# Scores in two passes, decay from two parts of g, later GpSimd constants and a store on a second queue: one hybrid attention layer

## Chip, cores and metric

One Trainium2 chip, one NeuronCore of it. The metric is the device time of one execution in microseconds (us); the kernel before has a median of 174.89 us over three runs (174.42 to 174.91).

## What is computed

One decoder layer on x of 256 tokens by 1024 columns, all in float32. After an RMS norm, one projection `h @ w_in` (1024 by 4104) gives ten parts. Eight softmax heads of 64 columns use the first four:

```
logit = q . k * 64**-0.5 - slope[h] * distance        # causal, 256 tokens
moba_out = softmax(logit) @ v * silu(a_z)
```

Four gated-delta heads of 128 columns use the rest. `g = -exp(a_log) * softplus(d_a + dt_bias)` is the log decay, `gc` its running sum, and `decay[i, j] = exp(gc[i] - gc[j])` for j not after i enters a triangular solve and a recurrence over the sequence. Both results, the second normed and gated, are joined and go through `w_out` (1024 by 1024); a last RMS norm and `x +` give the output.

## The kernel before, in words

**Precision by parts.** A float32 operand is split into a high part, rounded as it is written as float32r by ScalarE (ACT), and the low rest, made by VectorE (DVE). A product is then three TensorE (PE) passes of float32r: high by high, high by low, low by high. Weight groups of 512 columns come by DMA into four `raw` buffers, are split into `hi` and `lo` tiles (five buffers each), and feed the projections `dz`, `dk`, `dq`, `dv`, `av`, `aq`, `ak`, `az` and then `out` in that program order.

**The planner.** Nothing is emitted directly. Every operation is recorded (all have line 372 in the profile, so one goes by the tiles' names), and `Plan.run` list-schedules them by modelled durations; the best of eight rounds is the order in which each engine gets its instructions. `LEAD` is added to the priority of the operations of a stage; `BATCH` to that of a PE operation on the same rows as the one before it. Operations marked `late` (48 dummy `ps_warm` matmuls) go where the model finds PE without other work.

**The head** (L474 to L587). GpSimd (POOL) makes masks and other constants: `ident`, `ones`, `triu`, `blk`, `blks`, `strl`, `lvl`, `bias0`, `qscale`, zeros in `yz16` and in the `qz` tiles. For each half t of the tokens ACT squares 512 columns of x and DVE the other 512, each with a sum; DVE adds the two sums and EPS (L571); POOL raises that to -0.5 (L572, `raise_to`); ACT and DVE scale x (L573, L574); PE transposes it into `hT`, from which `hhi` and `hlo` are made. `dz` is the first projection.

**The decay** (L713 to L729). `gs` is `triu` times g of each head, 128 by 512 per chunk t, in float32. PE multiplies it by `strl` in float32 and adds the causal mask (`far16`, bf16) into `ps_d`; ACT makes `dT`, its exponential.

**The scores** (L976 to L1016). A query pair m has a tile `qz` with its high and its low part; each head e owns 64 of the 128 rows, and the other 64 are zeros written by POOL, so that PE contracts over 128 rows though only 64 count. The keys' parts `ka_h`, `ka_l` are 128 rows for both heads of a pair. Each head has two blocks of scores, of 128 and of 256 columns, and three matmuls for each:

```
PE.matmul(o, qh[:, ts], kh[:, m, ks], start=True, stop=False)
PE.matmul(o, qh[:, ts], kl[:, m, ks], start=False, stop=False)
PE.matmul(o, ql[:, ts], kh[:, m, ks], start=False, stop=True)
```

**The end** (L1102 to L1126). Squares and sums of `ps_out`, a power on POOL, then per column group a DVE operation and a store, all stores on SyncE's (SP's) queue: two groups for the first 128 tokens, three for the last 128.

Of the kernel before, what the change touches and what calls it, by code (L numbers as in the profile page):

```python
# [123 lines left out]
class Plan:  # L124
# [24 lines left out]
    def record(self, eng, real, name, args, kw):  # L149
        op = Op()  # L150
# [14 lines left out]
        after = kw.pop("after", False)  # L165
# [212 lines left out]
SLACK = 20  # L378

SWITCH = 90  # L380
BATCH = 0

MARGIN = [411, 175, 0]
TABLE = 2000
# [10 lines left out]
def tile_hybrid(  # L395
# [17 lines left out]
    plan = Plan()  # L413
# [4 lines left out]
    def const(shape, name, dtype=F32):  # L418
        return plan.tile(sb, shape, dtype, name)
# [4 lines left out]
    def sl(tag, shape, name, dtype=F32):  # L424
        return plan.tile(sb, shape, dtype, name, tag=tag)
# [14 lines left out]
    HD = D // 2  # L440
# [29 lines left out]
    HB = [P, HG, P]  # L470
# [9 lines left out]
    ones = const([P, P], "ones")  # L480
    G.memset(ones, 1.0)

    for t in range(NT):
        G.memset(yz16[:, of_chunk[t], :], 0.0)
# [4 lines left out]
    blk = const([P, NB, BASE], "blk")  # L489
    G.memset(blk, 1.0)  # L490
    G.affine_select(out=blk, in_=blk, pattern=[[-BASE, NB], [0, BASE]], compare_op=OP.is_ge,
                    fill=0.0, base=0, channel_multiplier=1)
    G.affine_select(out=blk, in_=blk, pattern=[[BASE, NB], [0, BASE]], compare_op=OP.is_ge,
                    fill=0.0, base=BASE - 1, channel_multiplier=-1)

    blks = const([P, NB, BASE], "blks")
    G.affine_select(out=blks, in_=blk, pattern=[[BASE, NB], [1, BASE]], compare_op=OP.is_gt,
                    fill=0.0, base=0, channel_multiplier=-1)
# [7 lines left out]
    V.tensor_scalar(far16, strl, -NEG, None, op0=OP.mult)  # L506
# [4 lines left out]
    nl = P // (2 * BASE)  # L511
    lvl = const([P, nl, 2, BASE], "lvl")
    G.memset(lvl[:, :, 0, :], 0.0)
    G.memset(lvl[:, :, 1, :], 1.0)
    G.affine_select(out=lvl[:, :, 1, :], in_=lvl[:, :, 1, :], pattern=[[-2 * BASE, nl], [0, BASE]],
                    compare_op=OP.is_ge, fill=0.0, base=0, channel_multiplier=1)
    G.affine_select(out=lvl[:, :, 1, :], in_=lvl[:, :, 1, :], pattern=[[2 * BASE, nl], [0, BASE]],
                    compare_op=OP.is_ge, fill=0.0, base=BASE - 1, channel_multiplier=-1)


    bias0 = const([P, P + T], "bias0")
    G.iota(bias0[:, :P], pattern=[[1, P]], base=0, channel_multiplier=-1,
           allow_small_or_imprecise_dtypes=True)
    G.affine_select(out=bias0[:, :P], in_=bias0[:, :P], pattern=[[-1, P]], compare_op=OP.is_ge,
                    fill=NEG, base=0, channel_multiplier=1)
    G.iota(bias0[:, P:], pattern=[[1, T]], base=-P, channel_multiplier=-1,
           allow_small_or_imprecise_dtypes=True)
    G.affine_select(out=bias0[:, P:], in_=bias0[:, P:], pattern=[[-1, T]], compare_op=OP.is_ge,
                    fill=NEG, base=P, channel_multiplier=1)
    slopes = [2.0 ** -(h + 1) for h in range(HA)]  # L530

    qscale = const([P, HA // 2], "qscale")
    for h in range(HA):
        b = DA * (h % 2)
        G.memset(qscale[b : b + DA, h // 2 : h // 2 + 1], (DA ** -0.5) / slopes[h])
# [29 lines left out]
    for t in range(NT):  # L565
        junk = sl(f"s{1 + t}", [P, D], f"xsq{t}")
        A.activation(junk[:, :HD], xs[t][:, :HD], AF.Square, scale=D ** -0.5, accum_out=ssq[:, t, 0:1])
        V.tensor_tensor_reduce(junk[:, HD:], xs[t][:, HD:], xs[t][:, HD:], 1.0 / D, 0.0, op0=OP.mult, op1=OP.add,
                               accum_out=ssq[:, t, 1:2])
        r = rx[:, t : t + 1]  # L570
        V.tensor_scalar(r, ssq[:, t, 0:1], ssq[:, t, 1:2], EPS, op0=OP.add, op1=OP.add)  # L571
        raise_to(r, r, -0.5, [P, 1])  # L572
        A.activation(xs[t][:, :HD], xs[t][:, :HD], AF.Copy, scale=r)  # L573
        V.tensor_scalar(xs[t][:, HD:], xs[t][:, HD:], r, None, op0=OP.mult)  # L574
# [409 lines left out]
    sm = const([P, HA, 2], "sm")
    rs = const([P, HA, 2], "rs")
# [4 lines left out]
    kps = proj_group(512, "ak")  # L990
    for half in range(2):
        plan.stage = f"att{half}"
        ps = qps[half]
        for c in range(2):
            m = 2 * half + c
            for e in range(2):
                b = slice(DA * e, DA * e + DA)
                qs_ = qscale[b, m : m + 1]
                qh, ql = qz[m][b, 0, e, :], qz[m][b, 1, e, :]
                A.activation(qh, ps[b, c, :], AF.Copy, scale=qs_)  # L1000
                V.scalar_tensor_tensor(ql, ps[b, c, :], qs_, qh, op0=OP.mult, op1=OP.subtract)
        ps = kps[half]
        hm = slice(2 * half, 2 * half + 2)
        A.activation(kh[:, hm, :], ps, AF.Copy)
        V.tensor_tensor(kl[:, hm, :], ps, kh[:, hm, :], OP.subtract)
# [102 lines left out]
    for t in range(NT):  # L1108
        n = len(groups[t])
        pq = tmp("pq", [P, n], f"pq{t}")  # L1110
        u = uu[:, t, :]
        r = tmp("pr", [P, 1], f"pr{t}")

        for i, (c0, cn) in enumerate(groups[t]):
            cs = slice(c0, c0 + cn)
            A.activation(osj[:, i % 2, :cn], accs[t][i], AF.Square, scale=D ** -0.5, accum_out=pq[:, i : i + 1])
            if i:
                V.tensor_scalar(r, pq[:, i : i + 1], r, None, op0=OP.add)
            else:
# [3 lines left out]
        for c0, cn in groups[t]:  # L1123
# [32 lines left out]
```

## Time and profile before

| | us |
|---|---|
| profiled execution | 174.88 |
| its span, first to last instruction | 172.9 |
| median of 3 runs | 174.89 |
| PE busy | 164.1 (95%) |
| DVE busy | 134.7 (78%) |
| ACT busy | 108.8 (63%) |
| POOL busy | 21.2 (12%) |

A matmul's own duration in the profile overlaps with the next one's, since they are pipelined; what PE needs for one is read from the distance of the starts, or from a piece of the chain of waits divided by its count. A float32 matmul shows as two records, a float32r or bf16 one as one. The shape shown for a matmul is that of the weights' rows and columns, then the moving operand's.

### The profile page before, as it was taken

Reading aid. Unit: us, or ns where it says so; the run is one execution under the profiler, and the core shown is the slowest. Engines: PE = TensorE matmul, PEld = TensorE weight load, DVE = VectorE, ACT = ScalarE, POOL = GpSimd, SP = SyncE. Lnnn points to the kernel's source line nnn. Section 1 sums busy time; section 2 is a strip of 40 time slices with the busy share of each in tenths; the row PEclk is TensorE's granted clock in tenths of the full one; section 3 lists DMA queues with packets and bytes.
Section 4 is the critical chain, followed back from the end, with each engine's and each line's share of the span. In section 5 each row is a group of like instructions: output and inputs, shape, how many; then the busy total and the mean of one; then the engine's idle time right before and its main releaser. Section 6 shows DMA issues by size and latency. Waiting matters only on the chain.

```text
span 172.9 us, 3465 instructions
## 1 busy us (share of the span) xinstructions
PE 164.1 (95%) x1311; PEld 154.1 (89%) x1311; DVE 134.7 (78%) x330; ACT 108.8 (63%) x231; POOL 21.2 (12%) x58
## 2 busy tenths in 40 slices
PE   7799999999999999999999999999999999999950
PEld 5589999997999999989999999999999998888850
DVE  4589566799579999898798999999689676474542
ACT  3689949968785545478554575665849594671230
POOL 8950000000000300400020000000001810000110
PEclk9999999999999999999999999999999999999995
DMA  5667689995776351067676108600000000640033
GB/s 193 232 224 261 224 271 241 391 317 136 207 233 161 91 189 57 5 205 276 222 245 200 69 0 251 238 0 0 8 0 4 2 0 0 196 172 0 3 118 121
DMA packets 12326, 24.92 MB, mean 144 GB/s; under 512 B 741, under 2 KB 1046, under 8 KB 12310
## 3 DMA queue, kind: packets, MB, share of 16 engines
q1 hardware_dynamic: 12310, 24.71, 44.1%
q8 instruction: 10, 0.16, 0.4%
q14 instruction: 6, 0.05, 0.1%
HBM read 23.65 MB, written 1.05 MB: 143 GB/s over the span
## 4 chain that ended last, share of the span: by engine, by line
PE 87%; POOL 5%; issue 4%; ACT 1%; DVE 1%; POOLq 0%; DVEq 0%
PE ps_out L372 10%; PE ps_av L372 9%; PE ps_az L372 7%; PE ps_dz L372 7%; PE ps_ak L372 7%; PE ps_dq L372 7%; PE ps_aq L372 7%; PE ps_dv L372 7%; PE ps_dk L372 7%; PE ps_s L372 3%; PE ps_y L372 2%; PE ps_w L372 2%; PE ps_gb L372 2%; PE ps_pt L372 2%; PE ps_d L372 1%
## 5 line engine op out<-in xcount | busy, mean ns | idle before, releaser
L372 DVE TENSOR_TENSOR o_lo<-raw_o,o_hi 128x1024 fp32r<-128x1024 f32 x8 | 9.8, 1220 | 5.1 <-ACT o_hi L372 5.1
L372 ACT ACTIVATE o_hi<-raw_o 128x1024 fp32r<-128x1024 f32 x8 | 8.4, 1056 | 5.0 <-PE ps_az L372 2.7
L372 ACT ACT_TABLE_LOAD x8 | 10.3, 1283 | 0.9 <-PEq L1143 0.8
L372 ACT ACTIVATE att_y<-att_y,mx 128x128 f32<-128x128 f32 (+1 forms) x16 | 7.2, 448 | 4.4 <-DVE mx L372 4.4
L372 PE MATMUL ps_az<-hlo,az_hi 128*128 128x256 f32 x32 | 9.8, 305 | 0.0
L372 PE MATMUL ps_az<-hhi,az_lo 128*128 128x256 f32 x32 | 9.6, 300 | 0.0
L372 PE MATMUL ps_aq<-hlo,aq_hi 128*128 128x256 f32 x32 | 9.6, 299 | 0.0
L372 PE MATMUL ps_az<-hhi,az_hi 128*128 128x256 f32 x32 | 9.5, 297 | 0.0
L372 PE MATMUL ps_warm<-wz 128*128 128x256 bf16 x48 | 8.3, 333 | 1.1 <-DVE wz L372 1.1
L372 PE MATMUL ps_aq<-hhi,aq_hi 128*128 128x256 f32 x32 | 9.3, 291 | 0.0
L372 PE MATMUL ps_aq<-hhi,aq_lo 128*128 128x256 f32 x32 | 9.2, 291 | 0.0
L372 PE MATMUL ps_dq<-hlo,dq_hi 128*128 128x256 f32 x32 | 9.1, 286 | 0.0
L372 PE MATMUL ps_dq<-hhi,dq_lo 128*128 128x256 f32 x32 | 9.1, 289 | 0.0
L372 PE MATMUL ps_ak<-hhi,ak_lo 128*128 128x256 f32 x32 | 9.1, 284 | 0.0
L372 PE MATMUL ps_ak<-hhi,ak_hi 128*128 128x256 f32 x32 | 9.1, 284 | 0.0
L372 PE MATMUL ps_dv<-hlo,dv_hi 128*128 128x256 f32 x32 | 9.1, 283 | 0.0
L372 PE MATMUL ps_dq<-hhi,dq_hi 128*128 128x256 f32 x32 | 9.0, 283 | 0.0
L372 PE MATMUL ps_dk<-hhi,dk_hi 128*128 128x256 f32 x32 | 9.0, 286 | 0.0
L372 PE MATMUL ps_dv<-hhi,dv_lo 128*128 128x256 f32 x32 | 9.0, 280 | 0.0
L372 PE MATMUL ps_ak<-hlo,ak_hi 128*128 128x256 f32 x32 | 9.0, 280 | 0.0
L372 PE MATMUL ps_dv<-hhi,dv_hi 128*128 128x256 f32 x32 | 9.0, 280 | 0.0
L372 PE MATMUL ps_dk<-hlo,dk_hi 128*128 128x256 f32 x32 | 8.9, 280 | 0.0
(254 smaller groups left out, 635.6 us busy)
## 6 DMA issues: line engine op xcount, KB each, us to landing
raw_o<-in_w_out_dram SPq DMA_DIRECT2D x4, 1024.0 KB, 5.0
raw_dz<-in_w_in_dram SPq DMA_DIRECT2D x8, 260.0 KB, 8.1
raw_dk<-in_w_in_dram SPq DMA_DIRECT2D x2, 1024.0 KB, 9.3
raw_dq<-in_w_in_dram SPq DMA_DIRECT2D x2, 1024.0 KB, 12.9
raw_dv<-in_w_in_dram SPq DMA_DIRECT2D x2, 1024.0 KB, 9.4
raw_av<-in_w_in_dram SPq DMA_DIRECT2D x2, 1024.0 KB
raw_aq<-in_w_in_dram SPq DMA_DIRECT2D x2, 1024.0 KB, 5.9
raw_ak<-in_w_in_dram SPq DMA_DIRECT2D x2, 1024.0 KB, 7.1
```

The costliest lines, as they stand in the source:

```text
L372: op.call(*args, **kw)
```

## The change

Six parts. The queries' high part of a head stays on its own 64 rows and its low part goes to the other 64; the keys' high part is written on both halves, so one matmul over 128 rows gives high by high and low by high together, and a second one with the keys' low part (zeros on the other half) the third product. `g` is split into two float32r parts, and the decay is two float32r matmuls for each chunk. POOL's constants that later stages use (`blk`, `blks`, `lvl`, `bias0`, `qscale`, the zeros in `yz16` and in the low keys) are the same operations as at the head before, now recorded after the `dz` stage, with a dependence on its last operation. The sum of the two square sums moves from DVE to POOL, with EPS as start of DVE's sum. The store of the second column group goes on ACT's queue. The planner's numbers are other ones.

```diff
-            op.preds[self.ops[-1]] = True
+            op.preds[after if isinstance(after, Op) else self.ops[-1]] = True
...
-BATCH = 0
+BATCH = 752
...
-LEAD = {"out0": 3258, "dk": 2097, "inv": -3594, "av": 2525, "dbl": -402, "out1": -1204, "att0": -470, "mixd": -508, "az": -1375}
+LEAD = {"out0": 3258, "dk": 12754, "inv": -3594, "dbl": -402, "out1": -1204, "att0": -192, "mixd": 1425, "az": -11589, "dz": -5411, "gates": 158, "vt": -3052}
...
-    strl = const([P, P], "strl")
+    strl = const([P, P], "strl", F32R)
...
-        V.tensor_tensor_reduce(junk[:, HD:], xs[t][:, HD:], xs[t][:, HD:], 1.0 / D, 0.0, op0=OP.mult, op1=OP.add,
+        V.tensor_tensor_reduce(junk[:, HD:], xs[t][:, HD:], xs[t][:, HD:], 1.0 / D, EPS, op0=OP.mult, op1=OP.add,
                                accum_out=ssq[:, t, 1:2])
         r = rx[:, t : t + 1]
-        V.tensor_scalar(r, ssq[:, t, 0:1], ssq[:, t, 1:2], EPS, op0=OP.add, op1=OP.add)
+        G.tensor_tensor(r, ssq[:, t, 0:1], ssq[:, t, 1:2], OP.add)
...
+    now = plan.ops[-1]
+    blk = const([P, NB, BASE], "blk")
+    G.memset(blk, 1.0, after=now)
+    G.affine_select(out=blk, in_=blk, pattern=[[-BASE, NB], [0, BASE]], compare_op=OP.is_ge,
+                    fill=0.0, base=0, channel_multiplier=1, after=now)
...
+    for t in range(NT):
+        G.memset(yz16[:, of_chunk[t], :], 0.0, after=now)
...
-    gsa = sl("ms", HBB, "gs")
+    gpart = [const(GS, f"g{i}", F32R) for i in "hl"]
+    A.activation(gpart[0], gneg, AF.Copy)
+    V.tensor_tensor(gpart[1], gneg, gpart[0], OP.subtract)
+    gsa = [sl(g, HBB, f"gs{g}", F32R) for g in ("ms", "wT")]
...
-        gs = gsa[:, of_chunk[t], :]
-        V.tensor_tensor(gs, triu[:, None, :].to_broadcast(HB), gneg[:, t, :, None].to_broadcast(HB), OP.mult)
-        PE.matmul(pd, strl, gs, start=True, stop=False)
+        for i in range(2):
+            gs = gsa[i][:, of_chunk[t], :]
+            V.tensor_tensor(gs, triu[:, None, :].to_broadcast(HB), gpart[i][:, t, :, None].to_broadcast(HB), OP.mult)
+            PE.matmul(pd, strl, gs, start=i == 0, stop=False)
...
+            G.memset(kl[own[1 - e], e, :].bitcast(F32), 0.0, after=now)
...
+    own = [slice(DA * e, DA * e + DA) for e in range(2)]
...
+            q, kh, kl = sets[m]
...
+                b, b2 = own[e], own[1 - e]
...
-                A.activation(qh, ps[b, c, :], AF.Copy, scale=qs_)
-                V.scalar_tensor_tensor(ql, ps[b, c, :], qs_, qh, op0=OP.mult, op1=OP.subtract)
-        A.activation(kh[:, hm, :], ps, AF.Copy)
-        V.tensor_tensor(kl[:, hm, :], ps, kh[:, hm, :], OP.subtract)
...
+                A.activation(q[b, e, :], ps, AF.Copy, scale=qs_)
+                V.scalar_tensor_tensor(q[b2, e, :], ps, qs_, q[b, e, :], op0=OP.mult, op1=OP.subtract)
+                ps = kps[half][b, c, :]
+                A.activation(kh[b, e, :], ps, AF.Copy)
+                A.activation(kh[b2, e, :], ps, AF.Copy)
+                V.tensor_tensor(kl[b, e, :], ps, kh[b, e, :], OP.subtract)
...
-                    PE.matmul(o, qh[:, ts], kh[:, m, ks], start=True, stop=False)
-                    PE.matmul(o, qh[:, ts], kl[:, m, ks], start=False, stop=False)
-                    PE.matmul(o, ql[:, ts], kh[:, m, ks], start=False, stop=True)
+                    PE.matmul(o, q[:, ts], kh[:, ks], start=True, stop=False)
+                    PE.matmul(o, q[:, ts], kl[:, ks], start=False, stop=True)
...
-            SP.dma_start(out[0, t * P : (t + 1) * P, cs], u[:, cs])
+            (AQ if i == 1 else SP).dma_start(out[0, t * P : (t + 1) * P, cs], u[:, cs])
```

## Rows read from the trace of the kernel before

**Rows 1.** The page's shares of the span by engine in the chain of work that ended last, and all that the view of waits gives for PE: who waited for whom, us in total, times, longest.

```profile
PE 87%; POOL 5%; issue 4%; ACT 1%; DVE 1%; POOLq 0%; DVEq 0%
PE hT L372 <- ACT x L372: 1.7, 2, 1.3
PE ps_warm L372 <- DVE wz L372: 1.1, 1, 1.1
```

**Rows 2.** Busy time of each engine in stretches of the span (start and end in us, the length, busy us and instructions of each engine, granted clock, DMA share, GB/s).

```profile
24.00:48.00 24.00, 24.00 (x195) 22.69 (x193) 19.34 (x41) 20.26 (x29) 0.00 (x0) 1.00 0.87 258
48.00:92.00 44.00, 44.00 (x333) 41.81 (x333) 40.00 (x93) 27.49 (x59) 4.60 (x5) 1.00 0.53 168
92.00:134.00 42.00, 42.00 (x425) 41.22 (x424) 38.91 (x115) 27.14 (x71) 0.76 (x4) 1.00 0.23 77
134.00:149.00 15.00, 15.00 (x115) 14.17 (x114) 9.06 (x19) 9.73 (x21) 4.46 (x9) 1.00 0.03 8
```

**Rows 3.** The chain of waits from 99 to 116 us: start, length, what.

```profile
103.30 0.70 PE ps_s L372 x6
...
108.77 0.53 PE ps_s L372 x5
...
110.27 1.02 PE ps_y L372 x32
```

**Rows 4.** PE in order of time: the decay's matmuls (start, length, what), and two neighbours of 512 columns in float32r.

```profile
40.52 1.02 PE L372 MATMUL ps_d<-gs,strl 128*128 128x512 f32 x2
41.38 0.38 PE L372 MATMUL ps_d<-far,ident 128*128 128x512 bf16 x1
...
159.55 0.40 PE L372 MATMUL ps_out<-o_lo,mixa_hi 128*128 128x512 f32 x1
159.78 0.39 PE L372 MATMUL ps_out<-o_hi,mixa_lo 128*128 128x512 f32 x1
```

**Rows 5.** POOL in order of time at the head.

```profile
5.52 0.99 POOL L372 MEMSET yz<- 128x512 f32 x2
6.47 0.57 POOL L372 TENSOR_TENSOR rx<-rx,pow-1_88 128x1 f32<-128x1 f32 x1
7.77 0.65 POOL L372 TENSOR_SCALAR_AFFINE_SELECT bias<-bias 128x128 f32<-128x128 f32 x2
8.39 1.08 POOL L372 TENSOR_TENSOR rx<-rx,pow-1_88 128x1 f32<-128x1 f32 x1
```

**Rows 6.** ACT and DVE in order of time at the head.

```profile
4.72 0.19 ACT L372 ACTIVATION_READ_ACCUMULATOR xsq<-x 128x1 f32 x1
5.00 0.21 DVE L372 TENSOR_SCALAR rx<-ssq 128x1 f32<-128x1 f32 x1
6.20 0.19 ACT L372 ACTIVATION_READ_ACCUMULATOR xsq<-x 128x1 f32 x1
7.07 0.72 ACT L372 ACTIVATE x<-x,rx 128x512 f32<-128x512 f32 x1 [0.69 <-POOL rx L372]
7.47 0.21 DVE L372 TENSOR_SCALAR rx<-ssq 128x1 f32<-128x1 f32 x1
9.51 0.72 ACT L372 ACTIVATE x<-x,rx 128x512 f32<-128x512 f32 x1 [0.55 <-POOL rx L372]
```

**Rows 7.** PE in order of time at the head.

```profile
7.85 1.16 PE L372 MATMUL hT<-ident,x 128*128 128x128 f32 x8 [1.29 <-ACT x L372]
10.44 1.13 PE L372 MATMUL hT<-ident,x 128*128 128x128 f32 x8 [0.39 <-ACT x L372]
...
23.87 0.72 PE L372 MATMUL ps_warm<-wz 128*128 128x256 bf16 x5
```

**Rows 8.** Groups of instructions by shape, on POOL, DVE and ACT: count, busy us, mean ns of one, idle before.

```profile
L372 POOL TENSOR_TENSOR om<-om,sq 128x4 f32<-128x4 f32 x4 | 0.8, 203 | 0.2
L372 POOL TENSOR_SCALAR_AFFINE_SELECT blks<-blk 128x128 f32<-128x128 f32 x1 | 0.8, 833 | 0.0
L372 DVE TENSOR_TENSOR gs<-triu,gneg 128x512 f32<-128x512 f32 x2 | 1.3, 683 | 0.0
L372 DVE TENSOR_TENSOR ka_l<-ps_ak,ka_h 128x512 fp32r<-128x512 f32 x2 | 1.4, 692 | 0.1
L372 DVE TENSOR_TENSOR u<-ps_out,wpost 128x256 f32<-128x256 f32 x2 | 0.8, 418 | 0.5 <-ACT osj L372 0.5
L372 ACT ACTIVATE avT<-ps_av 64x256 f32<-64x256 f32 x8 | 3.0, 372 | 2.5 <-PE ps_av L372 2.5
```

**Rows 9.** In order of time: ACT's last gate activations of `dz`, and DVE's first use of `blks`.

```profile
30.50 0.94 ACT L372 ACTIVATE zt<-ps_dz 128x256 f32<-128x256 f32 x3
...
63.20 1.28 DVE L372 TENSOR_TENSOR msk<-bT,blks 128x512 f32<-128x512 f32 x2
```

**Rows 10.** The end: PE's last matmul in order of time, and the last two pieces of the chain.

```profile
166.57 0.28 PE L372 MATMUL ps_out<-o_hi,mixa_lo 128*128 128x256 f32 x1
169.09 0.40 DVEq L1152
169.48 0.40 DVE u L372
```

**Rows 11.** The matmuls of `az` alone in a stretch (length, PE busy and count, clock, DMA share, GB/s), and DVE's making of their low parts, by shape.

```profile
100.00:134.00 34.00, 8.17 (x42) 1.00 0.19 64
L372 DVE TENSOR_TENSOR az_lo<-raw_az,az_hi 128x1024 fp32r<-128x1024 f32 x4 | 4.9, 1214 | 0.0
```

More of the change, by code (lines that the diff above doesn't have):

```diff
@@ L481, in tile_hybrid @@
     G.memset(ones, 1.0)
-    for t in range(NT):
-        G.memset(yz16[:, of_chunk[t], :], 0.0)
     triu = const([P, P], "triu")
@@ L487, in tile_hybrid @@
                     fill=0.0, base=0, channel_multiplier=-1)
[L489 to L498, printed above, removed]
-    strl = const([P, P], "strl")
+    strl = const([P, P], "strl", F32R)
     G.affine_select(out=strl, in_=ones, pattern=[[-1, P]], compare_op=OP.is_gt,
@@ L505, in tile_hybrid @@
     far16 = const([P, P], "far16", BF16)
-    V.tensor_scalar(far16, strl, -NEG, None, op0=OP.mult)
+    V.tensor_scalar(far16, strl.bitcast(F32), -NEG, None, op0=OP.mult)
     emod = const([P, BASE], "emod")
     V.tensor_reduce(emod, ident.rearrange("p (b k) -> p k b", k=BASE), op=OP.add, axis=AX.X)
[L511 to L535, printed above, removed]
     power = {}
@@ L668, in tile_hybrid @@
         A.activation(A_[t], z0[:, t, :], AF.Silu)
+    now = plan.ops[-1]
[3 more added lines that the diff above has]
+                    fill=0.0, base=0, channel_multiplier=1, after=now)
+    G.affine_select(out=blk, in_=blk, pattern=[[BASE, NB], [0, BASE]], compare_op=OP.is_ge,
+                    fill=0.0, base=BASE - 1, channel_multiplier=-1, after=now)
+    blks = const([P, NB, BASE], "blks")
+    G.affine_select(out=blks, in_=blk, pattern=[[BASE, NB], [1, BASE]], compare_op=OP.is_gt,
+                    fill=0.0, base=0, channel_multiplier=-1, after=now)
+    nl = P // (2 * BASE)
+    lvl = const([P, nl, 2, BASE], "lvl")
+    G.memset(lvl[:, :, 0, :], 0.0, after=now)
+    G.memset(lvl[:, :, 1, :], 1.0, after=now)
+    G.affine_select(out=lvl[:, :, 1, :], in_=lvl[:, :, 1, :], pattern=[[-2 * BASE, nl], [0, BASE]],
+                    compare_op=OP.is_ge, fill=0.0, base=0, channel_multiplier=1, after=now)
+    G.affine_select(out=lvl[:, :, 1, :], in_=lvl[:, :, 1, :], pattern=[[2 * BASE, nl], [0, BASE]],
+                    compare_op=OP.is_ge, fill=0.0, base=BASE - 1, channel_multiplier=-1, after=now)
+    bias0 = const([P, P + T], "bias0")
+    G.iota(bias0[:, :P], pattern=[[1, P]], base=0, channel_multiplier=-1,
+           allow_small_or_imprecise_dtypes=True, after=now)
+    G.affine_select(out=bias0[:, :P], in_=bias0[:, :P], pattern=[[-1, P]], compare_op=OP.is_ge,
+                    fill=NEG, base=0, channel_multiplier=1, after=now)
+    G.iota(bias0[:, P:], pattern=[[1, T]], base=-P, channel_multiplier=-1,
+           allow_small_or_imprecise_dtypes=True, after=now)
+    G.affine_select(out=bias0[:, P:], in_=bias0[:, P:], pattern=[[-1, T]], compare_op=OP.is_ge,
+                    fill=NEG, base=P, channel_multiplier=1, after=now)
+    slopes = [2.0 ** -(h + 1) for h in range(HA)]
+    qscale = const([P, HA // 2], "qscale")
+    for h in range(HA):
+        b = DA * (h % 2)
+        G.memset(qscale[b : b + DA, h // 2 : h // 2 + 1], (DA ** -0.5) / slopes[h], after=now)
+    for t in range(NT):
+        G.memset(yz16[:, of_chunk[t], :], 0.0, after=now)
     vh = const([P, NT, HA * DA], "vh", F32R)
@@ L975, in tile_hybrid @@
     avT = sl("s4", [P, HA // 2, T], "avT")
-    qz = [plan.tile(sb, [P, 2, 2, T], F32R, f"qz{m}", tag=g) for m, g in enumerate(("qz", "s3", "s2"))]
-    qz.append(qz[0])
-    for q in qz[:3]:
+    SET = [P, 2, 2, T]
+    q01 = const(SET, "qz", F32R)
+    k0, k1 = sl("s3", SET, "k0", F32R), sl("s2", SET, "k1", F32R)
+    qk2, kl2 = const(SET, "qk2", F32R), const([P, 2, T], "kl2", F32R)
+    sets = [(q01[:, 0], k0[:, 0], k0[:, 1]), (q01[:, 1], k1[:, 0], k1[:, 1]), (qk2[:, 0], qk2[:, 1], kl2)]
+    sets.append(sets[0])
+    own = [slice(DA * e, DA * e + DA) for e in range(2)]
+    for _, _, kl in sets[:3]:
         for e in range(2):
-            G.memset(q[DA * (1 - e) : DA * (2 - e), :, e, :].bitcast(F32), 0.0)
-    kh = const([P, HA // 2, T], "ka_h", F32R)
-    kl = const([P, HA // 2, T], "ka_l", F32R)
+            G.memset(kl[own[1 - e], e, :].bitcast(F32), 0.0, after=now)
     mx = const([P, HA, 2], "mx")
@@ L992, in tile_hybrid @@
         plan.stage = f"att{half}"
[L993 removed]
         for c in range(2):
             m = 2 * half + c
+            q, kh, kl = sets[m]
             for e in range(2):
[L997 to L1005 removed]
+                b, b2 = own[e], own[1 - e]
+                ps, qs_ = qps[half][b, c, :], qscale[b, m : m + 1]
+                A.activation(q[b, e, :], ps, AF.Copy, scale=qs_)
[4 more added lines that the diff above has]
+                V.tensor_tensor(kl[b, e, :], ps, kh[b, e, :], OP.subtract)
         for pr2 in range(2):
@@ L1010, in tile_hybrid @@
                 h = 2 * m + e
-                qh, ql = qz[m][:, 0, e, :], qz[m][:, 1, e, :]
+                q, kh, kl = (v[:, e, :] for v in sets[m])
                 ps_s = bank([P, P + T], f"ps_s{h}")
                 for o, ts, ks in ((ps_s[:, :P], slice(0, P), slice(0, P)), (ps_s[:, P:], slice(P, T), slice(0, T))):
-                    PE.matmul(o, qh[:, ts], kh[:, m, ks], start=True, stop=False)
-                    PE.matmul(o, qh[:, ts], kl[:, m, ks], start=False, stop=False)
-                    PE.matmul(o, ql[:, ts], kh[:, m, ks], start=False, stop=True)
+                    PE.matmul(o, q[:, ts], kh[:, ks], start=True, stop=False)
+                    PE.matmul(o, q[:, ts], kl[:, ks], start=False, stop=True)
                 y = tmp("att_p", [P, P + T], f"att_y{h}")
@@ L1122, in tile_hybrid @@
         raise_to(r, r, -0.5, [P, 1])
-        for c0, cn in groups[t]:
+        for i, (c0, cn) in enumerate(groups[t]):
             cs = slice(c0, c0 + cn)
             V.scalar_tensor_tensor(u[:, cs], u[:, cs], r, xr[:, t, cs], op0=OP.mult, op1=OP.add)
-            SP.dma_start(out[0, t * P : (t + 1) * P, cs], u[:, cs])
+            (AQ if i == 1 else SP).dma_start(out[0, t * P : (t + 1) * P, cs], u[:, cs])
     plan.emit(psum)
```

## The prediction

> **What bounds the kernel now.** I read first the chain that ended last and PE's waits. PE is 87% of the chain, and the only waits of PE that the profile finds are two at its very start, for the scaled x and for the dummy operand [rows 1]. Then I cut the span into stretches: from 24 to 149 us PE is busy without a gap [rows 2]. A busy PE alone proves little, as matmuls overlap in the records; what proves it is the distance of the starts, which the chain shows: six score matmuls in a row take 0.70 us, 32 small ones 1.02 us, and one group follows on the other [rows 3]. So the time is: the head until PE is fed, PE's queue, and a tail after the last matmul. What shortens PE's queue shortens the kernel, as long as nobody feeds PE later. The engine to watch is DVE: 38.91 of 42 us busy between 92 and 134 us, 40.00 of 44 before that, but only 9.06 of 15 behind it [rows 2]. ACT has room everywhere.
>
> The sum is made on the profiled execution, 174.88 us: its span of 172.9 and 2.0 around it, which I leave as it is. It lies 0.01 under the median, so no correction is needed.
>
> **Scores in two passes.** Eight heads times two blocks lose one matmul each: 16. In the chain, runs of five and six of them, half of 128 and half of 256 columns, take 0.53 and 0.70 us [rows 3], 0.106 to 0.117 us each. 16 x 0.117 = 1.87 us off PE; the low end by these rows is 16 x 0.106 = 1.70. The Trainium skill ("TensorE: Matmul & The Clock Gate", section "Back-to-back issue gap") gives about 81 ns for a sustained matmul of 128 columns and 109 ns for 256 by its formula; by that the part would be worth 8 x 0.190 = 1.52 us, an estimate from the page. The rows stand above it, and I go by the rows; by the page the result below would be 0.35 us later.
>
> **Decay.** A chunk's float32 product takes from 40.52 to 41.38 us, 0.86 us for its two records; a float32r matmul of 512 columns is 0.23 us from the next one's start [rows 4]. Two of these are 0.46, so each chunk saves 0.40 and both 0.80 us. The mask's matmul stays.
>
> **What these two parts add elsewhere.** For the decay DVE makes two more `gs` of 0.68 us [rows 8], one small subtraction of about 0.16 (as long as the 128x8 ones of the gates; between nothing and 0.21, the `rx` sum [rows 6]); ACT one small copy. That is 1.5 us of DVE near 37 us, in a stretch with 24.00 - 19.34 = 4.7 us of idle DVE [rows 2]; PE is fed by projections there, so I cost it at nothing. For the scores, per half, the one 128x512 `ka_l` of 0.69 becomes four on 64 rows by 256 columns. The nearest row, 256 columns out of PSUM, is 0.418 [rows 8]: 4 x 0.418 - 0.692 = 0.98, so 2.0 us more DVE in two halves. ACT gets eight copies of 0.372 per half for one 128x512 copy, so at most 6.0 us more in all [rows 8], beside 42 - 27.1 = 14.9 us of idle ACT [rows 2]: nothing. DVE is another matter. Its work from 92 to 134 us would be 38.9 + 2.0 = 40.9 us, while PE's, after the saving, is 42 - 1.87 = 40.1. Even with no gap at all DVE would now need 0.8 us more than PE in that stretch. Work for later stages can leave it, but such work feeds PE too. I take **0.8 us given back**; the low end is nothing (all of it moved behind 134 us, where DVE idles 5.9), the high end what comes out at DVE's density of before, 38.91/42 = 0.926: 40.9/0.926 = 44.2 us, 4.1 given back.
>
> **The head.** Before, the sum of squares of tile 0 is ready at 5.21, but POOL raises it to a power only at 6.47, behind two `yz` fills, and for tile 1 the DVE sum waits behind the scaling of tile 0 until 7.47 and POOL behind `bias` until 8.39 [rows 5, 6]. Without those constants: tile 0, accumulators read at 4.91, POOL's addition 0.20 (the 128x4 row [rows 8]), power 0.57, done near 5.8. ACT will likely square tile 1 first, which it reads out at 6.39 [rows 6], so scaling starts at 6.4 and not 7.07: 0.67 us. The other order would give 1.2. Tile 1: added by 6.65, power done near 7.3, scaling then and not at 9.51. PE's transposes start at 7.85 and go on at 10.44, with a hole between them that a few `dz` matmuls and dummies fill [rows 7]; of the hole I count 0.6, because from there ACT and DVE must deliver `hhi`, `hlo` and the split `dz` weights one after the other. The 48 dummies stay; 0.67 us less of waiting moves three of them into the time that counts (at 23.87 five lie in 0.72 us of which 0.28 is the last one's own length, so 0.11 each [rows 7]), 0.3 us. Together **0.9 us earlier**. Bounds: 0, if the weights' arrival sets the pace of `dz`, and 2.4, if all of tile 1's 2.2 us and the idle moments come through.
>
> **The moved constants** run after the last gate activation of `dz`, at 31.4 us, and `blks` is the first that is wanted, at 63.2 [rows 9]; POOL has nothing to do up to 48 [rows 2]. Cost nothing. If DVE had to stand still beside each of the seven that read what they mask (0.65 for two of `bias` [rows 5], 0.83 for `blks`, the longest [rows 8], four more below that), it would be under 4.8 us, about the 4.7 of idle DVE there [rows 2]. The seat of the addition on POOL is already in the head; nobody else waits in POOL's queue.
>
> **The store.** The third group's store stands behind the second on SP: DVE makes the last two one after the other, 0.40 us each, to 169.88 [rows 10], which leaves SP no more than an issue to catch up with: I count 0.1 us that goes when the second is on ACT's queue. What follows the issue stays. For the first tokens the store sits in ACT's queue ahead of the next squares, which wait for PE anyway. Bounds: 0.4 either way, one such step.
>
> **Planner's numbers.** `BATCH` keeps matmuls on the same rows together; the 32-row ones run 32 in a row already [rows 3]: nothing. `LEAD` for `dk` and `dz` moves splits of `dk` ahead at 20 us; `az` later by 10.2 us is the one with a price, treated below.
>
> Sum: -1.87 - 0.80 + 0.8 - 0.9 - 0.1 = -2.9, so 174.88 - 2.9 = **172.0 us**.
>
> **The rivals.**
> (1) *DVE does not bind and the head gives more.* For it: the postponed `az` takes 4 x 1.21 us of splits [rows 11] out of DVE's full stretch into its idle one. No give-back, and a head of 1.9 in place of 0.9: 172.0 - 0.8 - 1.0 = 170.2 us. Against it: `az` is the filler that PE has there.
> (2) *DVE becomes the bound at its old density.* 4.1 in place of 0.8 given back: 172.0 + 3.3 = 175.3, within 0.3% of before. For it: 93% of DVE's time was full with its dependences as they are. Against it: PE never waited for it, so the 7% idle may be just the slack.
> (3) *`az` starves, and the kernel is slower.* 42 of the `az` matmuls ran between 100 and 134 us, filling PE between the attention's small steps [rows 11]. With its priority 10.2 us lower, their splits on a nearly full DVE can stand behind all attention work; the rest of PE's work there waits for that same DVE. If all 42 find no place, PE has holes of 42 x 0.12 = 5.0 us (0.12 for a matmul of 256 columns, half of the 0.23 for 512 [rows 4] and a little) and does that work later: 172.0 + 5.0 = 177.0. It decides from 2.9 us of holes, some 24 matmuls, on. Against it: the scheduler gives PE whatever is ready, and attention's steps come earlier by what `az` gives up on DVE.
> (4) *The change does not do what it says:* should the new split of queries hold up each pair's first score, the 1.87 would go into a wait of PE for ACT or DVE. The first score of a half needs three ACT copies and two DVE steps on 64 rows, all of one head; before it needed one such copy and step for the query and two on 128 rows for the keys. So this has little for it, and its time is that of (2).
>
> **Chances.** Within 0.3% (0.5 us, about what a measurement of this kernel can tell from no change) counts as the same. Forecast 0.62, its own range 171.0 to 173.5 (head 0 to 1.5, give-back 0 to 1.5). Rival 1: 0.15. Rivals 2 and 4: 0.13. Rival 3: 0.10. Faster is forecast and rival 1, 0.77; same 0.13; slower 0.10. The range takes in the forecast and rival 1 with some more of the head, and leaves most of rivals 2 to 4 out: 169.8 to 174.3 us.
>
> **What would show it.** Right: `ps_s` with 32 records; `ps_d` with four float32r records 0.23 us apart; POOL's power for tile 1 ending before 7.6 us and the second transposes before 8.7; `dk` starting a microsecond earlier; no wait of PE in the view of waits after 12 us, and the last `ps_out` near 163.9 (166.9 before [rows 10]). Wrong: idle PE or stretched starts between 95 and 140 us, released by DVE (rivals 2, 3); `az` matmuls thinned out before 134 us with holes in place of them (rival 3); `dz` paced by its DMAs (head 0); PE's end unchanged though its work is less.

## The result: slower, and the profile after

The change made the kernel slower: 176.81 us (176.68 to 177.73) against 174.89, a ratio of 1.013 (1.009 to 1.017). I had forecast 172.0 in a range of 169.8 to 174.3, so the prediction was wrong in sign and outside its range. The profiled execution of after took 177.73 us, its span 176.0 against 172.9. It is the slowest of the four, 0.92 above their median, while that of before lies at its median; so the differences below are larger than those of the medians.

The page first: TensorE's granted clock in 40 slices, and the shares of the chain that ended last ([rows 1] has the chain of before).

```profile
PEclk9999999999999999999999999558999999999998
PE 74%; DVE 9%; ACT 6%; issue 5%; DMA 3%; SPq 1%; POOLq 0%; POOL 0%; DVEq 0%; ACTq 0%
```

Two things are new. Two slices, from 110 us on, are at half clock and the third, to 123 us, is at 0.8 in the mean, and PE has lost 13 points of the chain, most of them to DVE and ACT. The view of waits for PE has more than the two lines of [rows 1]:

```profile
PE ps_y L373 <- DVE xX L373: 0.6, 1, 0.6
PE hT L373 <- ACT hhi L373: 0.6, 1, 0.6
PE ps_w L373 <- DVE wT L373: 0.6, 1, 0.6
```

The stretches, with the columns of [rows 2]; the second of them is cut finer below it.

```profile
48.00:92.00 44.00, 43.90 (x324) 41.10 (x323) 41.47 (x101) 33.14 (x65) 3.56 (x3) 1.00 0.52 165
92.00:134.00 42.00, 40.78 (x371) 39.16 (x370) 36.62 (x108) 27.12 (x75) 2.87 (x8) 0.88 0.23 76
...
104.00:108.00 4.00, 3.34 (x53) 2.98 (x51) 3.94 (x9) 3.26 (x12) 0.61 (x2) 1.00 0.86 287
108.00:112.00 4.00, 3.44 (x44) 2.83 (x42) 3.91 (x13) 1.24 (x3) 0.00 (x0) 0.73 0.45 176
112.00:116.00 4.00, 4.00 (x26) 3.66 (x26) 2.59 (x8) 2.08 (x5) 0.00 (x0) 0.50 0.01 4
116.00:120.00 4.00, 4.00 (x21) 3.78 (x21) 2.39 (x10) 3.44 (x9) 0.00 (x0) 0.50 0.01 2
120.00:124.00 4.00, 4.00 (x43) 3.93 (x42) 2.94 (x11) 1.76 (x7) 0.00 (x0) 0.99 0.00 0
```

From 104 to 112 us DVE is full (7.85 of 8) and PE is not (6.78 of 8). From about 110 to 120 us the granted clock is 0.50, the lower level of 1.2 GHz: a mean of 0.73 over 108 to 112 us is 2.2 us of it at 0.50, so the fall began near 109.8. From 112 us on PE counts as busy throughout. What it did before the fall and after, in order of time:

```profile
104.69 0.28 PE L373 MATMUL ps_ak<-hhi,ak_hi 128*128 128x256 f32 x1
104.81 0.28 PE L373 MATMUL ps_ak<-hlo,ak_hi 128*128 128x256 f32 x1
...
106.82 1.24 PE L373 MATMUL ps_y<-xX,bT 32*32 32x32 f32 x32 [0.59 <-DVE xX L373]
...
108.96 0.69 PE L373 MATMUL ps_w<-wT,yz 32*32 32x32 f32 x16
109.57 0.76 PE L373 MATMUL ps_s<-k,qz 128*128 128x128 f32 x3
110.90 1.02 PE L373 MATMUL ps_w<-wT,yz 32*32 32x32 f32 x16 [0.56 <-DVE wT L373]
...
112.23 0.41 PE L373 MATMUL ps_ak<-hlo,ak_hi 128*128 128x256 f32 x1
112.44 0.41 PE L373 MATMUL ps_ak<-hhi,ak_lo 128*128 128x256 f32 x1
```

There are 64 matmuls of 32 rows by 32 columns, with two idle places of nearly 0.6 us. The fall comes behind the first of them and ahead of the second, which lies from 110.34 to 110.90 us. Behind both, two neighbouring `ps_ak` matmuls start 0.21 us apart, ahead of both 0.12. The chain through the same place is DVE's queue, one piece after the other (start, length, what):

```profile
104.17 1.12 DVE az_lo L373
...
105.33 0.70 DVE wT L373
...
106.68 0.67 DVE xX L373
...
109.30 0.43 DVE k L373
...
109.74 0.69 DVE vt L373
110.43 0.33 DVE wT L373
```

The head, against [rows 5] and [rows 7]: POOL's second power ends at 7.24 in place of 9.47, the second transposes start at 8.55 in place of 10.44.

```profile
6.69 0.55 POOL L373 TENSOR_TENSOR rx<-rx,pow-1_88 128x1 f32<-128x1 f32 x1
```

```profile
6.85 1.16 PE L373 MATMUL hT<-ident,x 128*128 128x128 f32 x8 [0.98 <-ACT x L373]
...
8.55 0.71 PE L373 MATMUL hT<-ident,x 128*128 128x128 f32 x4
```

The span splits at two starts: PE's first matmul of `dk` and its last `ps_out`.

| us | before | after | difference | forecast |
|---|---|---|---|---|
| to the first `dk` | 24.34 | 23.66 | -0.68 | -0.9 |
| `dk` to the last `ps_out` | 142.23 | 146.02 | +3.79 | -1.87 |
| from there to the end | 6.37 | 6.33 | -0.04 | -0.1 |

So head and tail did about what was said. The error is 5.7 us in the middle, where by the forecast PE had 2.67 us less to do; at the medians the whole error is 4.8 us, 176.81 against 172.0.

Some kernels below run with the fall of the clock in some executions and without it in others, and after had a fifth execution of 179.64 us at a mean clock of 0.955; such times are given apart, each with the mean granted clock.

### The profile page after: what moved, and what is told of

Read it like the earlier page. It is cut to its first block, busy times and chain, and to the rows that moved or that the text cites. A ratio compares the mean times of both kernels' runs of the same rounds, so it can differ in the third digit from the quotient of the medians.

```text
span 176.0 us, 3467 instructions
## 1 busy us (share of the span) xinstructions
PE 166.0 (94%) x1295; PEld 155.9 (89%) x1295; DVE 137.9 (78%) x337; ACT 112.6 (64%) x246; POOL 19.5 (11%) x60
## 4 chain that ended last, share of the span: by engine, by line
PE 74%; DVE 9%; ACT 6%; issue 5%; DMA 3%; SPq 1%; POOLq 0%; POOL 0%; DVEq 0%; ACTq 0%
PE ps_out L373 10%; PE ps_av L373 9%; PE ps_az L373 7%; PE ps_dk L373 6%; PE ps_dq L373 6%; PE ps_dv L373 5%; PE ps_dz L373 5%; PE ps_aq L373 5%; PE ps_ak L373 3%; DMA raw_dz<-in_w_in_dram 3%; DVE az_lo L373 2%; PE ps_gb L373 2%; PE ps_s L373 2%; ACT hhi L373 2%; PE ps_kq L373 2%
## 5 line engine op out<-in xcount | busy, mean ns | idle before, releaser
L373 PE MATMUL ps_aq<-hlo,aq_hi 128*128 128x256 f32 x32 | 9.1, 286 | 0.0
L373 PE MATMUL ps_dz<-dz_lo,hhi 128*128 128x264 f32 (+1 forms) x32 | 9.0, 296 | 0.0
L373 PE MATMUL ps_warm<-wz 128*128 128x256 bf16 x48 | 7.7, 315 | 1.1 <-DVE wz L373 1.1
```

Of the source, the lines that this page charges most:

```text
L373: op.call(*args, **kw)
```

## Experiments

A median stands with its lowest and highest run. Before ran beside all of them, at medians of 174.85 to 174.90.

**1. Is it the clock?** e1 fills the two idle places with dummies, written into a free part of a PSUM bank; e2 makes DVE lighter; e10 fills the first place alone.

```diff
+FILL = {"ps_y32": {0: 6}, "ps_w32": {8: 8}}   # e10: {"ps_y32": {0: 6}}
...
+            for _ in range(n_fill):
...
+                op.call(bank[:, 384 if scores else 256 :], *self.dummy(1 if scores else 2), start=True, stop=True)
...
+    plan.dummy = lambda n: (ident16.resolve(), far16[:, None, :].to_broadcast([P, n, P]).resolve())
```

> The changed kernel, same order on every engine, with 14 dummy bf16 matmuls added on PE where it stood idle: 6 of 256 columns ahead of the first 32-row ps_y (idle 0.6 us before), 8 of 128 columns ahead of the second half of the 32-row ps_w (idle 0.56 us). Theory A (the idle places let the granted clock fall to 0.5 from about 110 to 120 us, and that costs some 4 us): the clock stays at 1.0 in that stretch and the time is 172.3 to 173.8. Theory B (DVE paces this stretch and the clock costs little, since PE waits for DVE anyway): 176 to 178 whatever the clock does.

Measured: 174.53 us (174.37 to 174.96, ten runs), clock 0.988 to 0.997. In the stretches, against those of after above:

```profile
104.00:112.00 8.00, 7.72 (x111) 6.75 (x110) 7.82 (x20) 4.57 (x15) 0.61 (x2) 1.00 0.68 235
112.00:120.00 8.00, 8.00 (x84) 7.62 (x83) 7.13 (x27) 7.30 (x20) 0.00 (x0) 1.00 0.00 1
```

More work on PE gave a faster kernel: the clock stays at 1.00, and 2.3 us come back. That the fall costs at least this much is shown. But the time lies above the 172.3 to 173.8 that I expected of it, so the clock is not all.

> The kernel after with half of e1's filling: the 6 dummy matmuls ahead of the first 32-row ps_y stay, those ahead of the 32-row ps_w are gone. Theory A (the two waits of 0.6 us act together, either alone is covered by the work around it): clock 0.99 and 173.9 to 174.6. Rival B (the later wait, of ps_w on wT, is what lets the clock fall): clock 0.965 to 0.98 and 176.2 to 177.7, as after.

Measured: 176.95 (176.88 to 178.31), clock 0.965 to 0.977. The first place is filled, the second is left, and the fall is there:

```profile
PE ps_w L385 <- DVE wT L385: 0.7, 1, 0.7
```

```profile
112.00:120.00 8.00, 8.00 (x57) 7.37 (x55) 5.13 (x18) 6.53 (x18) 0.00 (x0) 0.57 0.00 1
```

The clock is 1.00 up to 112 us, so the fall now begins behind the second place. In after, where the first is open too, it had begun ahead of the second. So either place left open went with a fall, both filled with none, and my theory that only both together act fell.

```diff
-                V.tensor_tensor(kl[b, e, :], ps, kh[b, e, :], OP.subtract)
+                V.tensor_tensor(kl[b, e, :2], kps[half][b, c, :2], kh[b, e, :2], OP.subtract, cost=66 + 1.05 * 256)
```

The rest of the low keys is zeros, written by POOL.

> The changed kernel, same order on PE, DVE and ACT, but the low keys are made for 2 of their 256 columns only (the rest is zeros), which takes some 0.3 us from each of 8 DVE operations, 2.4 us in all. Theory C (the two-pass scores' extra DVE work starves PE and so drops the clock): no idle PE of more than 0.3 us near 106 and 110 us, clock 1.0, 171 to 173. Theory D (it is the order that the planner's new numbers make, not DVE's amount of work): the idle places and the fall of the clock stay, 175 to 177.

Measured: 172.59 in the one run at clock 0.997; the other five, at 0.956 to 0.975, took 175.6 to 178.5. One program, one order, and 3 to 6 us between its runs, which go with the clock. The profile is of a run of 175.61:

```profile
PE ps_w L373 <- DVE wT L373: 0.2, 1, 0.2
104.00:112.00 8.00, 7.69 (x100) 6.82 (x98) 7.75 (x23) 5.08 (x16) 0.57 (x2) 0.88 0.58 207
```

Of theory C the first half came, no idle place over 0.3 us, and the second did not: the clock fell in five of six runs. PE stands idle in this stretch for 0.31 us here and for 0.28 in e1, and the clock falls here and holds there. So shorter waits alone do not hold it; e1's dummies do.

**2. Planner's numbers or code?** e3 is the whole change with `LEAD` and `BATCH` of before; e4 the kernel before with the new numbers; e6 is after with `BATCH = 0` alone; e9 is e6 with dummies.

```diff
-BATCH = 752
+BATCH = 0
-LEAD = {"out0": 3258, "dk": 12754, ...}
+LEAD = {"out0": 3258, "dk": 2097, ...}        # e3 has both hunks, e6 the first, e4 both in reverse
```

> All of the change but the planner's numbers, which are those of before (LEAD, BATCH). Theory D (the new numbers' order is to blame): 171.5 to 173.5, faster than before, no fall of the clock. Theory C (the code's extra DVE work is to blame): the clock falls again or PE waits for DVE, 174.5 to 177.

Measured: 173.65 (173.59 to 173.91), ratio 0.993 (0.992 to 0.995), clock 0.993 to 0.997, no fall; just above theory D's range. This version beats both kernels and computes everything. But from `dk` to the last `ps_out` it is only 0.62 us shorter than before, with 2.67 us less on PE. The stretch from 92 to 120 us:

```profile
92.00:120.00 28.00, 26.80 (x280) 25.05 (x279) 27.13 (x77) 21.44 (x51) 2.76 (x2) 1.00 0.29 101
```

DVE is at 27.13 of 28, and PE, idle for 1.20 us, now has the slack.

> The kernel before with only the planner's new numbers (LEAD, BATCH). Theory D: slower than before, 176.5 to 180, with idle PE and a lower clock somewhere behind 95 us. Theory C: 174 to 176.

Measured: 178.29 (178.01 to 178.41), clock 0.989 to 0.998. Theory D's time came, its lower clock did not: without any fall the new numbers cost the old code 3.4 us, 1.2 of them before the first `dk` (25.52).

> The kernel after with one planner number put back: BATCH is 0 again, while the lead times LEAD stay new. Theory A (the fall of the clock belongs to the order that LEAD and BATCH make together, the late bursts of small matmuls beside a full DVE): either order is a new one; if the 32-row matmuls again meet waits of 0.5 us or more in 104 to 116 us, the granted clock falls there again and the time is 175.5 to 178; if not, 173.0 to 174.8. Rival B (BATCH alone spoils it): 173.0 to 173.9, as with the old numbers. Rival C (LEAD alone): 176 to 178, like after.

Measured, ten runs: 172.97 to 173.08 at clock 0.993 to 0.997 (three), 177.5 to 177.9 at 0.967 to 0.968 (five), 174.6 and 175.1 at 0.988 and 0.987. So the new `LEAD` is not slow in itself; its order is a fast one wherever the clock holds.

> The kernel of e6 (all of the change, BATCH 0, lead times new), same order, with 16 dummy bf16 matmuls put into TensorE's idle places: 4 of 256 columns ahead of the first 32-row ps_y, 12 of 128 columns ahead of the second part of the 32-row ps_w. Theory A (the idle places among the 32-row matmuls let the granted clock fall, and that is the whole of the 4.6 us between e6's runs): clock 0.99 or more in every run, no fall in 104 to 125 us, and 172.9 to 173.6 in each. Rival B (the clock falls for another reason, or at another place): runs at 0.968 and 177 to 178 appear again.

Measured: 173.89 (173.76 to 174.21), clock 0.989 to 0.991 in every run. In these four runs the dummies end the coin toss, at a price of 0.9 us against e6's undisturbed runs, which puts them above theory A's range.

**3. What sets the pace when the clock holds?** e5 is e3 with light keys, e16 is e1 with light keys (both leave out the low keys but for 2 of 256 columns); e11 puts e3's 16 saved matmuls back; e12 gives before more DVE work.

```diff
+            if op.eng == "pe" and op.args[0].buf.name in SCORES and kw["start"]:   # e11
+                op.call(*args, start=True, stop=True)
```

```diff
             op.call(*args, **kw)
+            if op.eng == "dve" and len(op.args) == 4 and getattr(op.args[0], "buf", None) is not None and op.args[0].buf.name in ("qz0", "qz1", "qz2", "qz3"):   # e12
+                op.call(*args, **kw)
```

> The whole change with the planner's numbers of before (as e3_old_numbers, 173.65), but the low part of the keys is made for 2 of its 256 columns only, so that 8 DVE subtractions shrink by about 0.3 us each, 2.4 us of DVE work taken out of the stretch from about 30 to 125 us; the order on TensorE, DVE and ScalarE is that of e3. Theory A (the two passes load DVE, and DVE is what now sets the pace from about 92 to 120 us): 171.0 to 172.6, DVE's busy time in 92 to 120 falls below 26.5 of 28 and the small waits of TensorE on att_y and the like close. Rival B (DVE is only beside the path, TensorE's own work and ScalarE set the pace with the old numbers): 173.3 to 173.8, not distinguishable from e3. Granted clock 0.99 or more under both.

Measured: 172.72 (172.33 to 173.19), a little above theory A's range. DVE has 26.55 of the 28 us from 92 to 120. The eight subtractions went from 0.42 to 0.15 us each: 0.93 us of time for 2.1 us of DVE.

> The kernel after with e1's dummies and e2's light low keys together (8 x 0.3 = 2.4 us less on DVE; the low keys are left out but for 2 of 256 columns): the clock held and DVE lighter. Theory A (DVE paces after's order from about 30 to 120 us): clock 0.99 or more in all runs and 172.4 to 173.2, against 174.5 of e1. Rival B (the dummies themselves cost about what e1 lacks): 173.8 to 174.5.

Measured: 173.18 (173.12 to 173.26), clock 0.988 to 0.998, as theory A has it: 1.35 us for the same 2.1 in the order of after.

> The kernel of e3 (all of the change, planner's numbers of before, 173.65), same order on all engines, with the first of each pair of scores matmuls run twice: the 16 matmuls that the two passes took away are back on TensorE, 16 x 0.117 = 1.87 us. Theory A (TensorE sets the pace in the scores with the old numbers, so its saving was worth what it measured): 175.2 to 175.7. Rival B (DVE sets the pace there, TensorE's saving fell into its small waits): 173.6 to 174.4.

Measured: 174.23 (174.10 to 174.63): 1.87 us of PE's work (16 x 0.117, an estimate from [rows 3]) cost 0.58. Theory A fell, B's time holds: what the two passes save on PE was mostly worth nothing in this order. That it went into waits is seen in part: from 92 to 120 us PE is idle for 1.20 us in e3 and for 0.79 in e11.

> The kernel before, same order, with the 8 DVE operations that make the query's low part run twice: 8 x 0.48 = 3.9 us more on DVE in about 84 to 122 us, nothing more on TensorE. Theory A (DVE is as full as TensorE there, 27.1 of 28 us busy in 92 to 120, so that work on it is paid): 176.5 to 178.8, with new waits of TensorE on DVE at 32-row matmuls or att_y. Rival B (DVE has slack of its own order, TensorE alone sets the pace before): 174.8 to 175.5. Rival C: as A, and the granted clock falls below 0.98: 178 or more.

Measured: 178.72 (178.71 to 178.83, three runs; 182.98 at clock 0.962 in a fourth): 3.9 us more on DVE made before 3.8 slower. Its waits and its stretch:

```profile
PE ps_y L372 <- DVE mx L372: 1.5, 1, 1.5
PE ps_y L372 <- DVE xX L372: 1.5, 1, 1.5
```

```profile
92.00:120.00 28.00, 24.76 (x257) 23.85 (x256) 26.97 (x68) 14.67 (x29) 0.00 (x0) 1.00 0.34 114
```

So DVE was level with PE already in before, behind a PE without a wait. The row also speaks against a simple rule for the clock: a wait of 1.51 us ahead of the 32-row `ps_y` left it at 1.00 in this profile.

**4. The parts.** e7 is the change without its two passes, e8 the two passes alone, both with the planner's numbers of before.

> The change without its two-pass scores and with the planner's numbers of before: decay from two parts of g, GpSimd's constants later and the last store on two queues stay, the scores are the three-pass ones of before. Theory A (of the 1.24 us that the change gains with old numbers, most is the head's 0.7 and the decay's 0.6, and the scores' saving on TensorE is given back by DVE): 173.2 to 173.9, about as e3. Rival B (the parts add up as TensorE's work: 0.7 of the head, 0.8 of the decay, and the scores' 1.87 are worth over 1): 174.0 to 174.6. Rival C, the decay's added parts cost waits: 174.9 or more.

Measured: 175.12 to 175.42 at clock 0.992 to 0.993 (three runs), 179.9 to 182.9 at 0.948 to 0.967 (six).

> The kernel before, planner's numbers too, with the two-pass scores alone (the query parts on 128 rows, 16 scores matmuls fewer, the high keys written twice, the low keys per half). Theory A (TensorE's 1.87 us are mostly given back, since DVE and ScalarE get work in the stretch where DVE is nearly full): 174.5 to 175.3, about no change. Rival B (the saving counts): 173.0 to 173.8. Rival C (the new order meets waits at 32-row matmuls and the granted clock falls below 0.98): 176 or more.

Measured: 175.18 to 175.38 at clock 0.988 to 0.993 (five runs), 176.3 to 177.3 at 0.971 to 0.981 (four), one of 181.8 at 0.948.

Each half alone loses 0.4 to 0.5 us with the clock held, both together (e3) gain 1.24. Each kernel is planned anew, so this doesn't price the halves, and that a new plan moves the time by as much as the parts do is likely but not shown apart. For the scores theory A's "about no change" holds with the clock held, and rival C's fall came in the other five runs. For the rest the time is rival C's, but the waits of PE in its profile are not at the decay, and why it gains nothing alone stays open.

**5. Can DVE be relieved?** e13 to e15 move the four `az_lo` subtractions to GpSimd, which is idle there, in after, before and e3; e17 moves e3's scaling of the probabilities to ScalarE, e18 for half of the heads, planned anew.

```diff
+            call = op.call
+            if op.eng == "dve" and isinstance(op.args[0], View) and op.args[0].buf.name in ON_POOL:
+                call = self.pool.tensor_tensor
+            call(*args, **kw)
...
+ON_POOL = ("az00_lo", "az01_lo", "az10_lo", "az11_lo")
```

> The kernel after, same order, with the four subtractions that make az_lo (128 x 1024, 1.2 us each on DVE, 4.9 us in all) on GpSimd, which is idle there. Theory A (a late DVE makes the two waits of 0.6 us among the 32-row matmuls, and these make the clock fall): both waits go or shrink below 0.3, no fall, 171.5 to 173.5. Rival B (the waits come from the order or from ScalarE): waits and fall stay, 176 to 178. Rival C (GpSimd's work slows DVE's by their shared access to memory, as GpSimd's om took 1.34 us beside DVE's o_lo instead of 0.23): DVE's own instructions in the stretch take longer, the waits stay, 176 or more.

Measured: 181.62 (177.71 to 184.70), clock 0.941 to 0.987.

> The kernel before, same order, az_lo's four subtractions (4.9 us of DVE) on GpSimd. Theory A (DVE is only level with TensorE in before: work added to it is paid, e12, but work taken from it gains nothing, since TensorE is 100% busy in 92 to 120): 174.3 to 175.1. Rival B (DVE paces before as well): 171.5 to 173.5. Rival C (contention): 175.5 or more.

Measured: 182.26 (179.14 to 182.34), clock 0.961 to 0.982.

> The change with the planner's numbers of before (e3, 173.65), same order, az_lo's four subtractions on GpSimd. Theory A (DVE paces, so that the 1.3 us of TensorE's saving that DVE holds back come free): 171.6 to 172.8, the best of all versions. Rival B (contention takes it back): 173.4 or more.

Measured: 181.18 (180.62 to 184.53), clock 0.949 to 0.972. The rivals with contention hold in all three: PE waits for DVE's `xX` for 3.0 us in e13, 2.4 in e14 and 5.1 in e15. The clock fell in all three profiles too, so the medians do not price the contention alone. DVE in e15, in order of time, while GpSimd made `az_lo` from 92.59 to 95.01 and from 95.36 to 102.71:

```profile
92.97 2.28 DVE L376 TENSOR_TENSOR wprod<-wc,gb 128x112 f32<-128x112 f32 x1
95.28 0.27 DVE L376 TENSOR_REDUCE wc<-wprod 128x8 f32<-128x112 f32 x1
95.59 2.44 DVE L376 TENSOR_TENSOR wprod<-wc,gb 128x120 f32<-128x120 f32 x1
...
100.86 3.00 DVE L376 TENSOR_TENSOR wT<-wc,blk 128x512 f32<-128x512 f32 x2
```

And the same instructions in e3:

```profile
93.20 0.36 DVE L373 TENSOR_TENSOR wprod<-wc,gb 128x112 f32<-128x112 f32 x1
93.60 0.27 DVE L373 TENSOR_REDUCE wc<-wprod 128x8 f32<-128x112 f32 x1
...
94.92 0.38 DVE L373 TENSOR_TENSOR wprod<-wc,gb 128x120 f32<-128x120 f32 x1
```

The operations with two SBUF operands stretch from 0.36 to 2.28 us, about the length of one GpSimd instruction (2.42); the reduction is as long as ever. So is an operation out of PSUM: in e13 `qz` took 0.49 us at 93.92, while GpSimd made `az_lo` from 91.26 to 96.23. Taking work from DVE in this way made DVE later.

> The kernel of e3 (173.65), order kept, with the 16 operations that scale the probabilities by the reciprocal sums (0.28 to 0.35 us each on DVE, 3.1 us in 88 to 124) on ScalarE. Theory A (DVE paces and ScalarE has room: 22 of 28 us busy in 92 to 120): 172.3 to 173.3, DVE's busy time in 92 to 120 below 26.5. Rival B (ScalarE's instructions of that form take some 0.4 us and it becomes late in its turn for yz and the high parts): 173.6 to 175.5, with TensorE waiting on ACT yz, att_pTh or k. Rival C (a new idle place among the 32-row matmuls drops the clock): 176 or more.

Measured: 174.45 to 174.79 at clock 0.985 to 0.995 (seven runs; the profiled one, in which the clock fell for about 3 us, 175.12), two of 176.9 and 178.3 at 0.973 and 0.964. The times are mostly rival B's, and C's in two. ScalarE took 0.50 us for the 256 columns that DVE scaled in 0.35, and PE waited for ScalarE, at the 32-row `ps_w` again:

```profile
PE ps_w L376 <- ACT yz L376: 0.7, 1, 0.7
```

> As e17, but planned anew and only for the four heads of the second half: 8 operations, about 2.5 us of DVE. Theory A (DVE paces): 172.6 to 173.4. Rival B (the new order meets idle places and the clock falls): 175 or more, with granted clock below 0.98. Rival C (ScalarE paces): 173.6 to 174.5.

Measured: 181.63 (180.24 to 182.03), clock 0.945 to 0.954, as rival B has it. The clock's row of the page:

```profile
PEclk9999999999999999999999999555599999999997
```

No move tried here beats e3.

## Why the prediction was wrong

- **Planner's numbers, "nothing": the step that failed.** I asked of `LEAD` and `BATCH` only which matmuls PE would have at hand, and priced them as work moved. They cost 3.2 us: the same code takes 173.65 with the numbers of before (e3), inside my range, and 176.81 with the new ones; the old code loses 3.4 by them (e4). In after most of it is the clock. The new order sets late DVE pieces ahead of the 32-row matmuls, PE stands idle for 0.59 and 0.56 us there, and the granted clock, which is 1.00 in every stretch of [rows 2], falls to 0.50 for some 10 us. I had no term for that. Nor does `BATCH` keep the 32-row matmuls together: `ps_w`, which ran as 32 in a row before, runs as 16 and 16. With the places filled it is 2.3 us less (e1), and this with dummies that cost something themselves: e16 took 173.18 with them, e2's one run at full clock 172.59 without, by which I estimate 0.6 for the dummies and 2.9 us for the fall. In e4 the clock held, so there the order costs its 3.4 us by itself.
- **Scores, -1.87, and DVE's give-back, +0.8.** The sixteen matmuls are gone from PE's queue (`ps_s` has 32 records), but the give-back was mis-sized, inside its stated bounds of 0 to 4.1. With the clock held (e1), `dk` to the last `ps_out` took 142.59 us, 0.36 more than before, though PE had 2.67 less: 3.0 came back, 2.4 without the dummies' estimated 0.6. With the numbers of before (e3) it was 2.05. That DVE is the reason is shown for 1.35 us of it (e16) and by e11 and e12; the rest is argued. I had DVE's 40.9 us against PE's 40.1 and took the difference, as though all of DVE's work could be dealt without a gap; DVE's idle time of before was no slack.
- **Decay, -0.80: right on PE.** A chunk's three matmuls run 0.23 us apart; the chain of e5 has them at 0.70 us each, against 0.86 and one more of 0.23 in [rows 4]. What it is worth in the end was not isolated (e7).

```profile
55.42 0.70 PE ps_d L373 x3
...
58.09 0.70 PE ps_d L373 x3
```

- **Head, -0.9:** 0.68, by the mechanism told: POOL's power for tile 1 at 7.24 (I said before 7.6), the second transposes at 8.55 (before 8.7). `dk` came 0.7 us earlier, not 1, and with the numbers of before (e3, 23.99) only 0.35.
- **The moved constants, "after the last gate activation of `dz`, at 31.4 us": misread.** The dependence on `dz` is one of the planner's list alone; on the chip POOL did not wait for it. It ran them right behind the second power, from 7.19 to 14.6 us, beside the work of the head. What they gave up is their place ahead of the powers, which is what the head needed; what they cost where they ran was not isolated.

```profile
7.19 0.20 POOL L373 MEMSET blk<- 128x128 f32 x1
...
12.17 1.19 POOL L373 TENSOR_SCALAR_AFFINE_SELECT bias<-bias 128x128 f32<-128x128 f32 x2
```

- **Store, -0.1:** 0.04 on PE's end to the span's end; no more than nothing.
- **Rival 3** (*`az` starves*) gave 177.0, next to what came, and 0.10 of chance. Its premise came true: the matmuls of `az` in its stretch fell from 42 [rows 11] to 22 (28 in e1, with the clock held; 52 in e3).

```profile
100.00:134.00 34.00, 5.36 (x22) 3.96 (x22) 0.00 (x0) 0.85 0.20 63
```

  But its price, 5.0 us of holes, did not: from 92 to 134 us PE is idle for 1.22 us in all, and e6, with the same lead times, takes 173.0 when the clock holds. The figure was right by accident.
- **Rival 2** (*DVE the bound at its old density*, 175.3) has the mechanism that is left when the clock is taken out, at a smaller price.
- **Rivals 1 and 4** did not come: the head gave 0.68 and not 1.9 and the give-back did not vanish, and PE has no wait at a score in the profile of after.

**What stays open:** what exactly lets the clock fall. Waits among the small matmuls do not settle it. In the profiles of after, e6, e10 and e17 it fell during or behind waits of 0.56 to 0.7 us at 32-row matmuls. But e5 (0.45 us, ahead of `ps_w`), e8 (0.66, ahead of `ps_y`) and e12 (1.51, ahead of `ps_y`) had such waits without a fall, and e2 had the fall with no wait over 0.2 us. e9 kept its wait of 0.7 us for `wT`, with 12 dummies behind it, and its clock.

## What to carry to other kernels

Where PE and a helper engine are both full, removing PE's work buys little: ask first what a microsecond more on the helper costs, which running some of its operations twice tells (here 3.8 us for 3.9). A planner's constants are part of the change: price the old code with the new constants and the new code with the old (here 3.4 and 3.2 us), and look at the granted clock's row before anything else. In this kernel the clock was lost at bursts of small matmuls that a late helper feeds; a few dummies there held it in all 14 runs (e1, e9), making the helper lighter did not (e2, five of six). Where the runs of a kernel fall in two groups by clock, such a place is worth looking for.

## What the runs showed of the hardware

- The granted clock of one core fell to 0.50 though PE, from 92 us up to the fall, was never idle for longer than 0.6 us (after) or 0.2 us (e2). The Trainium skill ("TensorE: Matmul & The Clock Gate", section "HAM oscillation — how this bites in real kernels") tells of long waits of TensorE, on DMAs, that bring the lower clock. Here the waits were short, and for DVE.
- Whether it falls can differ from run to run of one program: 172.97 to 173.08 us (clock 0.993 to 0.997) and 177.5 to 177.9 (0.967 to 0.968) in e6.
- GpSimd's 2.4 us `az_lo` held DVE's operations on two SBUF operands for 2.28 and 2.44 us (0.36 and 0.38 without) in e15, and no reduction (0.27 and 0.28). In e13 a DVE operation with one SBUF operand, `mx` of 128x2, took 2.02 us beside it (0.16 to 0.17 elsewhere). The Trainium skill ("Advanced Engine Details and Errata", section "GPSIMD Details") says that the two share a read and a write interface, and that DVE instructions with two SBUF inputs conflict, or those in a 2-port mode; for the first kind the trace agrees.
